# Making the low part of split weights with an accumulating DMA in two token mixers of a two-block transformer kernel

## The chip, the cores and the metric

The kernel runs on one core of one Trainium2 chip, as one launch. The metric is the device time in microseconds (us); lower is better. The engines are called PE (TensorE, matrix products), ACT (ScalarE), DVE (VectorE), POOL (GpSimd) and SP (SyncE, which here only issues DMAs). DMAs are also issued from POOL's and ACT's queues.

## What is computed

Two blocks follow on each other, on 256 tokens of 1024 features. All matrix products are wanted in float32 accuracy.

```python
def first_block(x, c, ctx, c_ctx, ...):      # two layers
    for l in range(2):
        mod = silu(c) @ w_mod[l] + b_mod[l]              # and the same for ctx
        h = rms_norm(x, g_pre_mix[l]) * (1 + sc1) + sh1  # layer 0: x and ctx, 512 tokens; layer 1: x, 256
        y = token_mixer(h, hc, ...)
        x = x + gt1 * rms_norm(y, g_post_mix[l])
        h = rms_norm(x, g_pre_ffn[l]) * (1 + sc2) + sh2
        x = x + gt2 * rms_norm(swiglu(h, w_ffn_in[l], w_ffn_out[l]), g_post_ffn[l])

def token_mixer(h, hc, ...):
    y_a = conformer_conv(h, w_in[:, :1024], ...)         # glu, depthwise convolution of width 31, layer norm
    y_b = differential attention of 8 heads, q, k and v from w_in, rotary positions
    y_c = multiscale_pool(h, w_in[:, 4096:4608], ...)
    g = sigmoid(h @ w_in[:, 4608:] + b_gate)
    return (g_a * y_a + g_b * y_b + g_c * y_c) @ w_out

def second_block(x, mem, positions, ...):    # two layers with other mixers and a swiglu each
```

## The kernel before

The streams lie in SBUF as 8 tiles [128 features, N tokens], with N = 512 in layer 0 of block 1 (x and ctx) and N = 256 from its layer 1 on. A product in float32 accuracy is made of three products in the faster type float32r. Each operand is split into a high part (the value rounded to float32r) and a low part (the value less its high part), and `mm3` (L160 to L166) runs high x high, high x low and low x high into the same PSUM tile. `lin` and `lin_deep` do so with the weights on the stationary side; `lin_nat` (L247 to L249) has them on the moving side.

The weights come as pieces of 128 partitions x 1024 elements, two to a load of 1 MB. `pieces` (L112) gives each piece a function `prep`. The prep of the first piece of a load issues the DMA into `raw`, a ring of two buffers of 1 MB (`RAWS`), from SP's queue (L124). Each prep then rounds its half of `raw` into a tile `whi` with ACT (L154) and writes `raw` less `whi` into a tile `wlo` (L155), on DVE or, for so many pieces in 8 as `SHARE` names for the phase, on POOL. The phase is 0 from the kernel's start to the end of layer 0's mixer, 1 in its ffn, 2 in layer 1's mixer, 3 in its ffn, and 4 to 7 in block 2. In phase 0 POOL subtracts 2 of 8 pieces, in phase 2 none.

Tiles `whi` and `wlo` lie in rings of four (`RING`). `emit` runs the steps of the whole kernel in order and calls a piece's `prep` as early as its ring allows, that is right after the step that uses the piece four before it for the last time. Some pieces of `w_out` in layer 0 use slots in place of the ring (`p.ring`), and some of block 2's weights are permuted (`perm`). Each engine's queue runs in order; the framework lays the queues out and sets all semaphores.

Around the weights a mixer's steps are: the glu's linears, then for four pairs of heads the linears of q, k and v merged with the attention of the pair before (`att_s` scores and softmax, L851 to L861; `att_t` transposes, L882 is the values' product of `att_v`; `rope` at L717 to L725) and with the taps of the convolution (L789 to L795: half of the channels on DVE, the other half scaled on ACT at L792 and added on POOL at L793). After that come the gates, the pooling branch, the output linears of the three branches and `w_out`. In layer 0 modulation products (L476, L478) run on DVE from further loads `mraw`.

Of the kernel before, what the change touches and what calls it, by code (L numbers as in the profile page):

```python
# [6 lines left out]
F32 = mybir.dt.float32  # L7
# [8 lines left out]
T = 256  # L16
# [10 lines left out]
SHARE = (2, 2, 0, 0, 4, 0, 0, 0)  # of 8 weight pieces, how many GpSimd subtracts, by phase  # L27
# [8 lines left out]
class Two:  # L36
    """[128, 8, n] in two tiles"""
# [8 lines left out]
class Kern:  # L46
# [22 lines left out]
    def static(self, tag, n, bufs, dt=F32):  # L69
        """the next of a ring of tiles [128, n] that lie in one"""  # L70
        if tag not in self.rings:
            self.rings[tag] = [self.cp.tile([128, n * bufs], dt, name=tag), 0]
        r = self.rings[tag]
        i = r[1] % bufs
        r[1] += 1
        return r[0][:, n * i:n * i + n]
# [4 lines left out]
    def brief(self, shape, dt=F32):  # L81
        """a small tile out of use before 32 more of its size are in"""
# [28 lines left out]
    def pieces(self, loads, na, nb, cuts, perm=False):  # L111
        box = {}  # L112
        out = []
        for i, (a0, a1, b0, b1) in enumerate(cuts):
# [3 lines left out]
            def prep(p=p, i=i, a0=a0, a1=a1, b0=b0, b1=b1):  # L118
                nc = self.nc
                if i == 0:  # L120
                    raw = self.static("raw", 2048, RAWS)
                    box["raw"] = raw[:, : na * nb].rearrange("p (a b) -> p a b", a=na)
                    for view, src in loads:
                        nc.sync.dma_start(view(box["raw"]), src)  # L124
# [43 lines left out]
    def lin(self, st, W, c0, ncols, rhs, N, evac, perm=False, K=8, tok=None, order=None):  # L168
        """out tile m [128, N] = W[r0:, c0 + 128 m : ...]^T rhs; rhs() -> [(hi, lo)] per k tile.
        tok: a range of the N tokens alone, which evac is told of"""  # L170
# [30 lines left out]
    def lin_pair(self, st, Wa, ca, Wb, cb, n, rhs, N, evac_a, evac_b):  # L201
        """tiles of two column ranges in turn, two by two"""
# [32 lines left out]
    def lin_nat(self, st, W, c0, lhs, ntok, evac):  # L235
        """out [128 tokens, 256 columns]; lhs(t) -> [(hi, lo)] per k tile, [128, 128 tokens]"""
# [50 lines left out]
    def sq_add(self, key, src, N, i, n):  # L287
        """adds src^2 to the running sum self.v[key]"""
# [12 lines left out]
    def col_rms(self, key, nt, dim):  # L301
        """sums over features (partitions) and then 1/rms per token: [128 tokens, nt]"""
# [9 lines left out]
    def bcast(self, r, nt, ps=None, at=0):  # L312
        """[128 tokens, nt] -> PSUM [128, 128 nt]: the same row of tokens on each partition"""
# [119 lines left out]
    def mod(self, l, g):  # L433
        """512 columns on the tensor engine: rows c, c_ctx of the high parts, then of the low parts"""
# [17 lines left out]
    def pin(self, inst):  # L452
        """keeps an instruction that waits for nothing from taking its tile far ahead of its turn"""
# [8 lines left out]
    def mod_v(self, st, l, groups, streams):  # L462
        """the same with the products and their sums over k tiles on the vector engine"""
# [52 lines left out]
    def pre_cols(self, l, s, gain):  # L516
        """(1 + scale) * gain for the two streams: [128, 8, 2]"""
# [13 lines left out]
    def acts(self, n, N):  # L531
        """hi and lo tiles for n k-tiles of N columns"""
# [11 lines left out]
    def act2(self, key, m):  # L544
        """tile m of a run of [128, 256] tiles, allocated two by two"""
# [4 lines left out]
    def norm_mod(self, i, t0, t1, rb, A, sh):  # L550
        """tile i of h from x for tokens t0..t1, whose 1 / rms starts at column 0 of rb"""
# [18 lines left out]
    def y_add(self, m, ps, tok, full):  # L570
        """a tile of the mixer's or the ffn's result: z = gate * gain * y, and the running sums over features of
        y^2, and if full of 2 x z and z^2; the last tile's terms stay apart"""
# [28 lines left out]
    def y_rms(self, t0, full):  # L601
        """1 / rms of y (and if full of the x to come) for 256 tokens: rows 0..255 (256..511) of a PSUM tile"""
# [36 lines left out]
    def residual(self, i, t0):  # L639
        """tile i of x += r * z for 256 tokens"""  # L640
# [7 lines left out]
    def next_h(self, gain):  # L648
        """block 2: the linears take gain * x; 1 / rms of the token follows behind them"""
# [12 lines left out]
    def ffn(self, st, Wgu, Wd, hs, N, evac, rb=None, mid=None):  # L662
        """rb: the tokens' 1 / rms, still missing in hs; the result then lacks it once"""
# [3 lines left out]
        for hi_, (f0, fn) in enumerate(halves):  # L667
# [37 lines left out]
            if mid and hi_ == len(halves) - 1:  # L705
                # by halves of the tokens, the last columns' weights split twice
# [1218 lines left out]
```

## Time and profile before

| | |
|---|---|
| time, median of 3 runs (least to most) | 2356.89 us (2349.86 to 2358.7) |
| profiled execution, first to last instruction | 2355.8 us |
| PE busy | 2197.7 us |
| DVE busy | 1707.7 us |
| ACT busy | 1095.3 us |
| POOL busy | 536.5 us |
| moved by DMA | 319.21 MB |

The profiled execution is one run; its span is what the traces are read against, and no separate time of it outside the profiler is given. Layer 0's mixer lies at about 60 to 615 us, its ffn up to about 1070 us, layer 1's mixer at about 1070 to 1450 us, its ffn up to about 1660 us, and block 2 behind that.

### The profile page before, as it was taken

How to read it: one execution, taken by the hardware profiler on the slowest of the kernel's cores; microseconds unless marked ns; L12 is line 12 of the kernel's file. 1: busy time of each engine (PE TensorE's matmuls, PEld its weight loads, DVE VectorE, ACT ScalarE, POOL GpSimd, SP SyncE). 2: the span in 40 equal slices, each digit the busy share in tenths (PEclk: the TensorE clock that was granted, in tenths of full speed). 3: DMA queues.
4: the chain of work that ended last, by engine and by line, in shares of the span. 5: the costliest groups of instructions: out<-in, count | busy, mean ns of one | idle time of the engine just before them, and what ended most of it. 6: DMA issues, size and time to landing. Idle time of an engine off the chain costs nothing.

```text
span 2355.8 us, 37801 instructions
## 1 busy us (share of the span) xinstructions
PE 2197.7 (93%) x14576; PEld 1998.8 (85%) x14576; DVE 1707.7 (72%) x3443; ACT 1095.3 (46%) x2110; POOL 536.5 (23%) x545
## 2 busy tenths in 40 slices
PE   4978889999989999989999899999889999999998
PEld 3767777788888888878788899999877999988998
DVE  5697987959678745578988877764686766686665
ACT  5436565332332222244566554554446544465543
POOL 2344433321340110143333312100342000210000
PEclk8989999999999999998999999999987999999999
DMA  7312112335414555553322454455541555542553
GB/s 271 93 55 67 54 59 72 123 132 170 152 63 154 168 179 170 170 165 108 108 72 90 148 174 160 154 193 176 160 90 37 176 183 177 177 144 84 185 180 125
DMA packets 296628, 319.21 MB, mean 135 GB/s; under 512 B 20544, under 2 KB 264352, under 8 KB 296448
## 3 DMA queue, kind: packets, MB, share of 16 engines
q1 hardware_dynamic: 293072, 311.27, 41.1%
q0 software_dynamic: 2224, 3.43, 0.6%
q8 instruction: 114, 1.87, 0.3%
q10 hardware_dynamic: 1152, 2.10, 0.3%
q14 instruction: 66, 0.54, 0.1%
HBM read 315.72 MB, written 1.05 MB: 134 GB/s over the span
## 4 chain that ended last, share of the span: by engine, by line
PE 66%; DVE 21%; issue 4%; ACT 3%; DMA 3%; POOL 1%; SPq 0%; ACTq 0%; DVEq 0%; POOLq 0%
PE p L164 19%; PE p L165 19%; PE p L166 19%; DVE wlo L155 3%; DVE t L795 3%; DVE t L478 2%; DVE t L258 2%; PE p L742 1%; DVE b L851 1%; DMA mraw<-in_w_mod_dram 1%; DVE t L725 1%; PE tr L484 1%; DMA raw<-in_w_in_dram 1%; PE p L247 1%; ACT whi L154 1%
## 5 line engine op out<-in xcount | busy, mean ns | idle before, releaser
L164 PE MATMUL p<-t,whi 128*128 128x256 f32 (+1 forms) x3724 | 1175.5, 320 | 20.8 <-ACT t L560 8.5
L165 PE MATMUL p<-t,whi 128*128 128x256 f32 (+1 forms) x3724 | 1183.0, 319 | 5.6 <-DVE t L561 2.1
L166 PE MATMUL p<-t,wlo 128*128 128x256 f32 (+1 forms) x3724 | 1178.2, 318 | 6.4 <-DVE wlo L155 4.8
L164 PEld LDWEIGHTS p<-t,whi 128*128 128x128 f32 x3724 | 718.8, 195 | 72.6 <-ACT t L560 10.3
L165 PEld LDWEIGHTS p<-t,whi 128*128 128x128 f32 x3724 | 723.6, 194 | 50.8 <-DVE t L659 3.5
L166 PEld LDWEIGHTS p<-t,wlo 128*128 128x128 f32 x3724 | 723.1, 194 | 50.4 <-DVE wlo L155 5.9
L154 ACT ACTIVATE whi<-raw 128x1024 fp32r<-128x1024 f32 (+4 forms) x487 | 492.0, 1020 | 543.4 <-PE p L165 332.6
L155 DVE TENSOR_TENSOR wlo<-raw,whi 128x1024 fp32r<-128x1024 f32 (+4 forms) x443 | 545.4, 1232 | 201.7 <-ACT whi L154 113.7
L155 POOL TENSOR_TENSOR wlo<-raw,whi 128x1024 fp32r<-128x1024 f32 (+2 forms) x44 | 103.5, 2353 | 503.6 <-ACT whi L154 464.8
L478 DVE SCALAR_TENSOR_TENSOR t<-mraw,big,t 128x512 f32<-128x512 f32 x224 | 176.6, 827 | 17.7 <-DMA mraw<-in_w_mod_dram 16.2
L793 POOL TENSOR_TENSOR t<-t,t 128x512 f32<-128x512 f32 (+1 forms) x120 | 134.9, 1125 | 186.0 <-ACT t L792 178.5
L594 POOL TENSOR_TENSOR t<-t,t 128x256 f32<-128x256 f32 (+1 forms) x68 | 70.4, 1063 | 246.1 <-ACT t L596 242.8
L299 POOL TENSOR_TENSOR t<-t,t 128x256 f32<-128x256 f32 (+1 forms) x27 | 25.6, 948 | 430.6 <-ACT t L297 430.1
L260 ACT ACTIVATE t<-t 128x256 fp32r<-128x256 f32 (+1 forms) x115 | 54.3, 473 | 148.9 <-DVE t L689 104.4
L742 PE MATMUL p<-t,t 64*128 64x256 f32 (+2 forms) x528 | 78.5, 374 | 28.5 <-DVE t L261 9.8
L247 PE MATMUL p<-whi,t 128*128 128x256 f32 x352 | 101.8, 289 | 2.8 <-ACT t L853 1.6
L248 PE MATMUL p<-wlo,t 128*128 128x256 f32 x352 | 99.8, 284 | 0.0
L249 PE MATMUL p<-whi,t 128*128 128x256 f32 x352 | 99.8, 283 | 0.0
L689 DVE TENSOR_TENSOR t<-t,p 128x256 f32<-128x256 f32 (+1 forms) x91 | 43.1, 474 | 76.8 <-PE p L166 76.6
L795 DVE SCALAR_TENSOR_TENSOR t<-u,big,t 128x512 f32<-128x512 f32 (+1 forms) x120 | 94.9, 791 | 1.5
L742 PEld LDWEIGHTS p<-t,t 64*128 64x128 f32 x528 | 50.9, 206 | 49.2 <-issue 16.8
L257 ACT ACTIVATE t<-t 128x256 fp32r<-128x256 f32 (+1 forms) x92 | 43.2, 495 | 100.0 <-DVE t L725 80.6
(299 smaller groups left out, 2717.0 us busy)
## 6 DMA issues: line engine op xcount, KB each, us to landing
raw<-in_w_in_dram SPq DMA_DIRECT2D x60, 1024.0 KB, 5.1
raw<-in_l_w_gate_up_dram SPq DMA_DIRECT2D x44, 1024.0 KB, 5.1
raw<-in_w_ffn_in_dram SPq DMA_DIRECT2D x42, 1024.0 KB, 5.3
mraw<-in_w_mod_dram SPq DMA_DIRECT2D x80, 512.0 KB, 4.0
raw<-in_l_w_in_dram SPq DMA_DIRECT2D x15, 1024.0 KB, 5.2
raw<-in_l_w_down_dram SPq DMA_DIRECT2D x16, 896.0 KB, 4.9
t<-in_w_mod_dram SPq DMA_DIRECT2D x32, 256.0 KB, 5.4
raw<-in_w_attn_out_dram SPq DMA_DIRECT2D x8, 1024.0 KB, 5.2
```

Of the source, the lines that this page charges most:

```text
L154: nc.scalar.activation(p.hi, src, AF.Copy)
L155: eng.tensor_tensor(p.lo, src, p.hi, op=ALU.subtract)
L164: mm(ps, lh, rh, start=first, stop=False)
L165: mm(ps, lh, rl, start=False, stop=False)
L166: mm(ps, ll, rh, start=False, stop=last)
L247: mm(ps[:, :256], lh, p.hi[:, k % 4], start=k == 0, stop=False)
L248: mm(ps[:, :256], lh, p.lo[:, k % 4], start=False, stop=False)
L249: mm(ps[:, :256], ll, p.hi[:, k % 4], start=False, stop=k == 7)
L478: nc.vector.scalar_tensor_tensor(acc, w[:, k], c, acc, op0=ALU.mult, op1=ALU.add)
L742: self.nc.tensor.matmul(out[half], q[i // 2][h, qs], k[i % 2][h, ks], start=i == 0, stop=i == 2)
L793: nc.gpsimd.tensor_tensor(acc, acc, t, op=ALU.add)
L795: nc.vector.scalar_tensor_tensor(acc, u, w, acc, op0=ALU.mult, op1=ALU.add)
```

## The change

In phases 0 and 2 a piece that has a load of one DMA, the ring of `whi` and `wlo`, and no permutation is prepared in another way. Its load is cut into one DMA for each piece, which writes the piece's weights as one run of 4 KB in each partition of `raw`. ACT writes minus the rounded weights into `wlo` (scale -1), a DMA from POOL's queue adds `raw` to `wlo` in place, and ACT then rounds the weights into `whi` in a second pass. No subtraction is left for these pieces, and the count for `SHARE` does not go on.

```diff
+BY_DMA = (0, 2)
...
                     box["raw"] = raw[:, : na * nb].rearrange("p (a b) -> p a b", a=na)
-                    for view, src in loads:
-                        nc.sync.dma_start(view(box["raw"]), src)
+                    box["dma"] = self.phase in BY_DMA and len(loads) == 1 and not p.ring and not perm
+                    if box["dma"]:
+
+                        at = 0
+                        box["run"] = []
+                        for c0, c1, d0, d1 in cuts:
+                            n = (c1 - c0) * (d1 - d0)
+                            box["run"].append(raw[:, at:at + n])
+                            nc.sync.dma_start(raw[:, at:at + n].rearrange("p (a b) -> p a b", a=c1 - c0),
+                                              loads[0][1][:, c0:c1, d0:d1])
+                            at += n
+                    else:
+                        for view, src in loads:
+                            nc.sync.dma_start(view(box["raw"]), src)
+                if box["dma"]:
+                    src = box["run"][i]
+                    n = src.shape[1]
+                    hi = self.wp.tile([128, 1024], F32R, name=self.nm("whi"), tag="whi", bufs=RING)
+                    lo = self.wp.tile([128, 1024], F32R, name=self.nm("wlo"), tag="wlo", bufs=RING)
+
+                    nc.scalar.activation(lo[:, :n], src, AF.Copy, scale=-1.0)
+                    nc.gpsimd.dma_start(lo[:, :n].bitcast(F32), src, accum_op=ALU.add)
+                    nc.scalar.activation(hi[:, :n], src, AF.Copy)
+                    p.hi = hi[:, :n].rearrange("p (a b) -> p a b", a=a1 - a0)
+                    p.lo = lo[:, :n].rearrange("p (a b) -> p a b", a=a1 - a0)
+                    return
                 src = box["raw"][:, a0:a1, b0:b1]
```

## Rows read from the trace of the kernel before

**Rows 1.** Busy times of the page: busy us, share of the span, instructions.

```profile
PE 2197.7 (93%) x14576; PEld 1998.8 (85%) x14576; DVE 1707.7 (72%) x3443; ACT 1095.3 (46%) x2110; POOL 536.5 (23%) x545
```

**Rows 2.** Busy time of each engine by stretch (from:to, length, then the engines).

```profile
core 0: us, PE busy (x) PEld busy (x) DVE busy (x) ACT busy (x) POOL busy (x), PEclk, DMA share, GB/s
...
110.00:450.00 340.00, 303.07 (x1686) 250.51 (x1685) 291.42 (x571) 176.62 (x401) 140.57 (x106) 0.96 0.20 66
450.00:615.00 165.00, 164.02 (x780) 136.70 (x779) 128.66 (x176) 52.54 (x67) 28.03 (x15) 0.99 0.52 163
...
1110.00:1345.00 235.00, 216.25 (x1523) 197.49 (x1521) 209.92 (x466) 136.02 (x298) 80.06 (x114) 0.96 0.31 101
1345.00:1450.00 105.00, 104.48 (x867) 103.66 (x866) 75.69 (x130) 60.81 (x105) 19.89 (x20) 1.00 0.55 179
```

**Rows 3.** The same for L155, the subtractions: DVE, then POOL.

```profile
110.00:450.00 340.00, 41.96 (x30) 26.27 (x11) 0.96 0.20 66
...
1110.00:1345.00 235.00, 56.91 (x43) 0.00 (x0) 0.96 0.31 101
1345.00:1450.00 105.00, 44.08 (x37) 0.00 (x0) 1.00 0.55 179
```

**Rows 4.** The same for L154, the rounding on ACT.

```profile
110.00:450.00 340.00, 42.11 (x40) 0.96 0.20 66
450.00:615.00 165.00, 29.26 (x28) 0.99 0.52 163
...
1110.00:1345.00 235.00, 46.14 (x44) 0.96 0.31 101
1345.00:1450.00 105.00, 36.16 (x35) 1.00 0.55 179
```

**Rows 5.** Waits of PE, 110 to 450 us: us in total, times, longest.

```profile
PE tr L869 <- DVE t L861: 10.1, 10, 1.8
...
PE tr L925 <- DVE t L923: 0.8, 1, 0.8
```

**Rows 6.** Waits of PE, 1110 to 1345 us.

```profile
PE tr L869 <- DVE t L861: 9.2, 5, 3.8
PE p L164 <- ACT t L260: 3.4, 1, 3.4
...
PE tr L925 <- DVE b L269: 0.2, 1, 0.2
```

**Rows 7.** DMA queue 1, and DMA issues with size and median us to landing.

```profile
q1 hardware_dynamic: 293072, 311.27, 41.1%
...
raw<-in_w_in_dram SPq DMA_DIRECT2D x60, 1024.0 KB, 5.1
...
mraw<-in_w_mod_dram SPq DMA_DIRECT2D x80, 512.0 KB, 4.0
...
t<-in_mem_dram POOLq DMA_DIRECT2D x4, 256.0 KB, 3.5
...
t<-in_k_axc_dram POOLq DMA_DIRECT2D x1, 128.0 KB, 2.3
```

**Rows 8.** Busy times in the first stretches, as in rows 2.

```profile
20.00:30.00 10.00, 8.16 (x34) 6.42 (x34) 7.50 (x13) 5.31 (x12) 1.86 (x5) 1.00 1.05 387
30.00:40.00 10.00, 5.25 (x28) 4.42 (x27) 4.50 (x21) 10.00 (x27) 0.00 (x0) 0.70 1.06 381
```

**Rows 9.** Timeline of DVE and POOL: start, us, instruction.

```profile
1387.10 1.23 DVE L155 TENSOR_TENSOR wlo<-raw,whi 128x1024 fp32r<-128x1024 f32 x1 [2.18 <-ACT whi L154]
...
1258.85 1.67 DVE L155 TENSOR_TENSOR wlo<-raw,whi 128x1024 fp32r<-128x1024 f32 x1
...
1258.71 0.73 POOL L719 TENSOR_TENSOR t<-t,t 128x256 f32<-128x256 f32 x1 [3.34 <-DVE t L717]
```

**Rows 10.** A plain DMA's issue on POOL: ns least, median, most.

```profile
L1301 POOL DMA_DIRECT2D t<-in_mem_dram x4: 543/548/621, 1336.5 to 1338.1; - x4
```

## The prediction, made before the changed kernel ran

> **What bounds the kernel now.** I read the page's busy times first. TensorE (PE) is busy for 93% of the span, VectorE (DVE) for 72% [rows 1]. A share over the whole span hides the stages, so the second view is the table of busy times by stretch, cut at the two mixers that the change touches [rows 2]. The reader should see two kinds of stretch there.
>
> In the first kind, the attention parts (110 to 450 us of layer 0, 1110 to 1345 us of layer 1), PE has gaps: 340 - 303.1 = 37 us and 235 - 216.3 = 19 us. DVE is the busiest engine beside it, 291.4 of 340 us (86%) and 209.9 of 235 us (89%). In the second kind, the dense parts (450 to 615 and 1345 to 1450 us), PE has no gap worth naming: 1.0 and 0.5 us. Nothing that is taken off DVE there can be won.
>
> The third view says whom PE waits for. In 110 to 450 us nine rows name DVE, 35.1 us in all, from 10.1 down to 0.8 us [rows 5]. In 1110 to 1345 us six rows name DVE, 15.5 us in all, and one names ScalarE (ACT), 3.4 us [rows 6]. The releasers are softmax, rope and split instructions, not the weights' own subtraction (2.1 us at most among the six). So the subtractions do harm by standing in DVE's in-order queue ahead of those instructions. About 35 + 15 = 50 us is therefore all that a lighter DVE can give back.
>
> The fourth view is the DMA share by stretch, since the change adds transfers. It is 0.20 and 0.31 in the attention parts, 0.52 and 0.55 in the dense ones [rows 2].
>
> **The change part by part.** From the steps' order about 170 pieces of 128 x 1024 weights take the new path: some 85 in layer 0's mixer (which has phase 0 from the start of the kernel, and whose last steps prepare four pieces of the ffn behind it) and some 85 in layer 1's.
>
> *Removed: the subtraction.* In the attention part of layer 0 DVE loses 42.0 us in 30 instructions and GpSimd (POOL) 26.3 us in 11; in that of layer 1 DVE loses 56.9 us in 43 [rows 3]. A POOL instruction beside it stretches a DVE one: the subtraction took 1.67 us while a POOL addition ran, 1.23 us alone [rows 9]. POOL's 11 subtractions go as well, and at 0.44 us each DVE gets some 4 us more. DVE falls from 86% to (291.4 - 46) / 340 = 72%, and from 89% to (209.9 - 56.9) / 235 = 65%. Its free share goes from 14 to 28% and from 11 to 35%. I take it that a wait behind a queue shrinks about as the free share grows: a half of 35.1 us remains, and a third of 15.5 us. That gives -18 and -10 us. The bounds are 0 (the waits are the length of a chain and not a queue) and -35 and -15.5 us. The start of layer 1's mixer, before 1110 us, still prepares its first four pieces the old way and the next ones the new way: -2 us.
>
> *Added: a second pass of ACT over each piece,* at the price of the pass that is there: 42.1 us / 40, 46.1 / 44, 36.2 / 35, so 1.05 us [rows 4]. ACT goes from 176.6 to 219 of 340 us, from 136.0 to 182 of 235 us, and from 60.8 to 97 of 105 us in layer 1's dense part. Layer 0 has room. In layer 1's attention part PE's 3.4 us of waiting for ACT [rows 6] about doubles: +3 us (bounds 0 and +8). In the dense part ACT is 92% full and still fits. The rounded part now comes 1.05 us later than before, and three pieces of PE time are in hand there (below).
>
> *Added: the accumulating DMA.* No row of before shows one, so its three prices are bounded from plain transfers. First, its issue: POOL's DMA instructions take 0.55 us [rows 10], so 85 of them are 47 us for each layer. That is about what POOL loses in layer 0 and is spread over layer 1, where POOL has 80.1 of 235 us [rows 2]. A POOL instruction behind it waits until the minus pass has been done; these are conv additions and rope additions of a later tile, so I put it at nothing. If that cover fails, a rope addition is late and q or k behind it.
>
> Second, its latency. On the POOL queue 128 KB took 2.3 us and 256 KB 3.5 us to land; on the SP queue 512 KB took 4.0 and 1024 KB 5.1 us [rows 7]. For 512 KB of accumulation I take 4 to 6 us. The low part is then ready 1.05 + 0.55 + 4 to 6, so 5.6 to 7.6 us after the minus pass begins. With rings of four, that pass may begin when the piece four before is used up, three pieces ahead. In the tightest place, the 105 us with 36 pieces (35 and 37 instructions in [rows 3, 4]), a piece takes 2.9 us and the lead is 8.7 us. So it fits, with 1 to 3 us to spare. The rows say little on a POOL transfer of this size. The Trainium skill's page "DMA: Bandwidth & Descriptors" (section "Anatomy of one DMA — SWDGE (gpsimd) path") fits such a DMA as 2.0 us plus its bytes over 436 GB/s; an estimate from that page for 512 KB is 3.2 us, less than the 3.5 us that this trace has for half as much, so the row decides.
>
> Third, its share of the 16 DMA engines. Queue 1 moved 311.27 MB in 41.1% of 2355.8 us [rows 7]: 1.6 us for each 512 KB of plain load. The dense part of layer 1 agrees, 0.55 x 105 / 36 = 1.6 us for each piece. A piece there lasts 2.9 us. Bounds for the accumulation are 0 (it runs beside the loads unseen) and 3.2 us (it reads two operands, each at the price of a load). I take the plain transfer, 1.6 us: 128 rows of 4 KB between two places in SBUF should not be dearer than a load in 1 KB pieces, and the second operand's read may be covered. Then load and accumulation need 3.2 us, and about 40 pieces (36 and the four of the ffn behind them) are 0.3 us late each: +12 us. With 0 it is 0, with 3.2 us it is 40 x (4.8 - 2.9) = +76 us. In layer 0's dense part the DMA engines have 0.52 x 165 = 86 us of work and get 28 x 1.6 = 45 us more. That fits into 165 us: 0 (at 3.2 us, 176 us: +11). In the attention parts 0.20 x 340 + 40 x 1.6 = 132 of 340 us and 0.31 x 235 + 44 x 1.6 = 143 of 235 us fit; at 3.2 us, 214 us still fits.
>
> *Moved: the loads.* Each 1 MB load becomes two of 512 KB in runs of 512 B where they were 1 KB, and the buffer is free only when the accumulation has landed. Two more issues for each pair of pieces are of no weight on a queue that issues one load each 5.8 us here. The loop of a raw half then is: load 4.0, minus pass 1.05, issue 0.55, landing 4 to 6, so 9.6 to 11.6 us against four pieces of 2.9 us = 11.6 us. Closed just in time; nothing is added, and this is the second place where it may fail.
>
> *The start.* Four pieces go the new way in the first 45 us, where the DMA share reaches 1.05 [rows 8]: four passes of ACT of 1.05 us and 4 x 1.6 = 6.4 us of transfers, against four subtractions less. Bounds 0 and +8; I take +2.
>
> The sum: -18 - 10 - 2 + 3 + 12 + 2 = -13 us. The profiled span of 2355.8 us becomes 2343 us, and as the median of the runs lies 1.1 us above that span, the forecast is 2344 us.
>
> **The rivals.** *The DMA engines become the bound.* This ends on the other side. The profile shows for it that a dense piece of layer 1 has only 2.9 - 1.6 = 1.3 us of DMA time free; against it, that stretches with 381 to 387 GB/s exist [rows 8], more than the 179 of the dense part [rows 2] even with the accumulation's bytes added once. Its price is 3.2 us in place of 1.6: -30 + 3 + 76 + 11 + 8 = +68 us at the most, and with some overlap of the two queues about +50: 2407 us. It decides from where the accumulation costs more than about 1.9 us of all engines: 40 x (1.6 + 1.9 - 2.9) = 24 us eats the gain. The Trainium skill's page "Collectives: The Full Stack" (Part 3, "The bandwidth ceiling") says just this: an add inside a DMA costs nothing as arithmetic, but needs two source reads on one read queue and so ran at half the rate of a copy. No row of before shows an accumulation, so the trace neither agrees nor disagrees; because of that rule the rival has a chance as high as it has.
>
> *The waits are chains.* PE's waits for DVE are mostly one instruction long (10.1 us in ten waits, [rows 5]); if they come from softmax steps that follow on each other, a shorter queue gives little, say -12 in place of -30, and the costs of 17 us stay: 2362 us.
>
> *The accumulation is hidden.* With 0 to 1.3 us of engine time nothing is added in the dense part: -30 + 3 + 2 = -25, so 2332 us.
>
> *The low parts come late.* If landing takes 9 us under load, the raw loop is 14.6 us, so 0.75 us for each of 40 pieces: -13 + 30 = +17, 2374 us.
>
> *It does not do what it says* (most pieces would keep the old path): the condition is one load, no ring of slots, no permutation, and only block 2's weights are permuted. I leave it no chance of its own.
>
> **How the numbers follow.** Forecast 0.38, hidden 0.14, chains 0.14, DMA bound 0.28, late 0.06. A measurement of this kernel can tell about 0.5% from no change, 12 us. Around the forecast (2330 to 2356 us) about 0.28 of the 0.38 lies under 2345 us. Faster: 0.28 + 0.14 = 0.42. The same: 0.10 + 0.14 + 0.02 = 0.26. Slower: 0.28 + 0.04 = 0.32. The range reaches from 2318 us (hidden, with two thirds of the waits gone) to 2410 us (the DMA-bound case), leaving out the ends of both. The forecast's own range is 2330 to 2356 us.
>
> **What would show it.** The subtraction should be gone from DVE and POOL in both mixers, and ACT's passes over raw doubled, near 1.05 us. PE's waits for DVE should fall to about 17 and 5 us in the attention parts. In layer 1's dense part the DMA share should rise from 0.55 to above 0.9, and PE should begin to wait for wlo by about 0.3 us a piece. If the DMA share is 1 and PE waits for wlo or raw by 1 us and more a piece, the accumulation reads twice. If the accumulating DMA lands later than 8 us, its latency decides. If PE's waits for DVE stay near 35 us, they were chains. Slower attention parts would prove me wrong outright.

## The result and the profile after

The changed kernel takes 2451.61 us (median; 2447.19 to 2456.9), the kernel before 2354.97 us in the same set of runs: a ratio of 1.0419 [1.04, 1.0438], 96.6 us slower. The forecast was 2344 us with a range up to 2410 us, so both the sign and the range were wrong. The two profiled executions, which all readings below are made from, are 2355.8 and 2445.0 us long, 89.2 us apart.

Line numbers of after lie 25 higher for the old code (`mm3` is L189 to L191, the softmax's last step L886, the transposes L894, the modulation's split L282 and its matmuls L472 and L473, the gates' tanh L934, two other splits L285 and L1059). In the other kernels all lines shift by a few. New lines: L132 the load of one piece, L144 the minus pass, L145 the accumulating DMA, L146 the rounding.

The page's busy times, then the two DMA queues, then the groups of the new lines (count | busy us, mean ns of one | idle before them, and what ended it), then two rows of DMA issues (size and median us to landing). They answer to [rows 1, 7, 10].

```profile
PE 2218.8 (91%) x14576; PEld 2013.3 (82%) x14576; DVE 1494.4 (61%) x3298; ACT 1249.8 (51%) x2280; POOL 604.5 (25%) x690
...
q1 hardware_dynamic: 367120, 311.27, 40.8%
q0 software_dynamic: 26704, 92.05, 20.4%
...
L145 POOL DMA_DIRECT2D wlo<-raw x170 | 149.0, 882 | 403.3 <-ACT wlo L144 354.4
L144 ACT ACTIVATE wlo<-raw 128x1024 fp32r<-128x1024 f32 x170 | 177.7, 1046 | 46.9 <-DMA raw<-in_w_in_dram 27.6
...
wlo<-raw POOLq DMA_DIRECT2D x168, 512.0 KB, 6.4
raw<-in_w_in_dram SPq DMA_DIRECT2D x116, 512.0 KB, 5.9
```

DVE has lost 213 us of work, as was meant, and the new pass of ACT costs what was taken, 1.05 us. The new thing is queue 0, which in before is nearly empty (queue, kind: packets, MB, share of 16 engines):

```profile
q0 software_dynamic: 2224, 3.43, 0.6%
```

20.4% of 2445.0 us less 0.6% of 2355.8 us is 485 us, so one accumulation of 512 KB takes as much time of the DMA engines as all 16 have in 485 / 170 = 2.85 us. Its issue holds POOL for 0.88 us, not 0.55, and it lands after 6.4 us.

Busy times by stretch of after, cut at the same stages as [rows 2] (columns as there):

```profile
core 0: us, PE busy (x) PEld busy (x) DVE busy (x) ACT busy (x) POOL busy (x), PEclk, DMA share, GB/s
130.00:470.00 340.00, 311.59 (x1719) 257.98 (x1719) 237.04 (x548) 219.41 (x449) 146.58 (x146) 0.97 0.59 133
470.00:655.00 185.00, 184.33 (x911) 155.17 (x910) 92.39 (x154) 86.53 (x108) 38.87 (x41) 1.00 1.00 250
1150.00:1375.00 225.00, 212.01 (x1510) 193.81 (x1510) 160.37 (x406) 171.28 (x336) 106.44 (x144) 0.98 0.88 200
1375.00:1540.00 165.00, 128.75 (x912) 123.94 (x910) 31.14 (x85) 95.21 (x144) 48.73 (x63) 0.88 1.04 235
```

The last row is where most of the time went. PE does there in 165 us little more than what took it 105 us before (912 instructions against 867), and the DMA share has gone from 0.55 to 1.04. (The share adds up the packet times of all queues, 64.7% and 39.0% for the two large ones below, so it can pass 1.) The 36.3 us in which PE is idle are told by its waits in that stretch (us in total, times, longest); the waits of ACT and SP, from their own answers, are behind them:

```profile
PE p L191 <- DMA wlo<-raw: 18.4, 15, 2.5
PE p L189 <- ACT t L934: 10.2, 1, 10.2
PE p L189 <- ACT t L1059: 3.8, 1, 3.8
PE p L189 <- ACT t L285: 3.4, 1, 3.4
...
ACT whi L146 <- DMA raw<-in_w_in_dram: 29.3, 6, 13.9
ACT whi L146 <- DMA raw<-in_w_out_dram: 14.0, 6, 5.1
...
SPq L132 <- DMA wlo<-raw: 148.3, 37, 8.4
```

Read from below: SP stands 148 of 165 us until an accumulation lets go of its raw buffer; the load that it then issues is late; ACT stands at the rounding until the load lands; and PE waits for the low part, or for a tanh that stands behind the rounding in ACT's queue. That SP stands is no sign by itself, as it issues each load as soon as a buffer is free. In before it stands too, and there it waits for DVE's subtractions, for instance, in the 135 us from 1345 to 1480 us:

```profile
SPq L124 <- DVE wlo L155: 75.2, 14, 11.3
```

What is new is that the load then comes too late for ACT. One step of the loop in after (start us, length, instruction; idle time before it and what ended it) shows this, and also that the framework has put the rounding (L146) ahead of the minus pass (L144) here; in the whole stretch L146 waits for a load 17 times and L144 three times. So the accumulation begins one pass later than the code reads:

```profile
1467.83 1.06 ACT L146 ACTIVATE whi<-raw 128x1024 fp32r<-128x1024 f32 x1 [4.42 <-DMA raw<-in_w_in_dram]
...
1469.15 1.05 ACT L144 ACTIVATE wlo<-raw 128x1024 fp32r<-128x1024 f32 x1
...
1470.50 0.86 POOL L145 DMA_DIRECT2D wlo<-raw  x1 [5.92 <-ACT wlo L144]
```

The rest of the 60 us is PE itself: its mean instruction took 128.75 / 912 = 0.141 us, 0.1205 us in [rows 2]; on 912 instructions that is 19 us. The granted clock is 0.88 there, a mean between its two levels of 1.2 and 2.4 GHz, in place of 1.00.

The DMA queues of the same stretch (busy tenths of the engines in 40 slices, then the queues, then size and median us to landing of the accumulations and of the largest group of loads; the other groups of loads lie between 5.4 and 7.5 us):

```profile
DMA  9999999989999999999999999999999999999995
...
q0 software_dynamic: 5568, 19.86, 64.7%
q1 hardware_dynamic: 34445, 18.69, 39.0%
...
wlo<-raw POOLq DMA_DIRECT2D x35, 512.0 KB, 7.5
raw<-in_w_in_dram SPq DMA_DIRECT2D x12, 512.0 KB, 8.1
```

Queue 0 moved 19.86 MB, so 38 accumulations of 0.524 MB, and 64.7% of 165 us is 107 us: 2.8 us for each. The price is the same where the engines are full.

To place the whole loss, the starts of five instructions that every kernel here has are read from each trace (lines of before): the first tile of h (L560, the end of the start), the first addition of the convolution's layer norm (L921, right behind the last softmax, once for each layer), the last modulation product of layer 0 (L478), and the last tile of h for layer 1's ffn (L560). The stretches between them, in us:

| kernel | start | attention, layer 0 | dense and ffn, layer 0 | attention, layer 1 | dense, layer 1 | the rest |
|---|---|---|---|---|---|---|
| before | 61.5 | 329.9 | 677.7 | 242.3 | 172.1 | 872.3 |
| after | 86.6 | 329.4 | 686.2 | 239.7 | 232.4 | 870.7 |
| change | +25.1 | -0.5 | +8.5 | -2.6 | +60.3 | -1.6 |

The last column warns of how exact this is: no experiment changes how weights are prepared there (some have a third raw buffer or fewer slots), and it came out between 859.6 and 872.3 us over all of them. So a difference under some 5 us in one stretch is not read, unless the timed comparison bears it out.

The start, last. SP's issues in after (start us, length, instruction), then in before, then one wait of ACT and one of PE in after:

```profile
1.93 6.02 SPq L132 DMA_DIRECT2D raw<-in_w_in_dram  x3
8.40 32.60 SPq L464 DMA_DIRECT2D t<-in_w_mod_dram  x32
41.35 6.41 SPq L132 DMA_DIRECT2D raw<-in_w_in_dram  x4
```

```profile
1.92 1.99 SPq L124 DMA_DIRECT2D raw<-in_w_in_dram  x2
14.46 19.93 SPq L439 DMA_DIRECT2D t<-in_w_mod_dram  x32
```

```profile
ACT wlo L144 <- DMA raw<-in_w_in_dram: 19.1, 1, 19.1
...
PE p L472 <- ACT t L282: 28.8, 7, 18.7
```

In before both 1 MB loads, with the first four pieces, stand ahead of the 32 modulation loads. In after three half loads do, and the fourth comes behind all 32. ACT's queue has the minus pass of that fourth piece ahead of most splits of the modulation weights, so ACT stood 19.1 us for it, and PE 28.8 us for those splits, 6.6 us in before.

### The profile page after: what moved, and what is told of

Same layout as the page of the kernel before. It is cut to its first block, busy times and chain, and to the rows that moved or that the text cites. A ratio compares the mean times of both kernels' runs of the same rounds, so it can differ in the third digit from the quotient of the medians.

```text
span 2445.0 us, 38384 instructions
## 1 busy us (share of the span) xinstructions
PE 2218.8 (91%) x14576; PEld 2013.3 (82%) x14576; DVE 1494.4 (61%) x3298; ACT 1249.8 (51%) x2280; POOL 604.5 (25%) x690
## 3 DMA queue, kind: packets, MB, share of 16 engines
q1 hardware_dynamic: 367120, 311.27, 40.8%
q0 software_dynamic: 26704, 92.05, 20.4%
HBM read 315.72 MB, written 1.05 MB: 130 GB/s over the span
## 4 chain that ended last, share of the span: by engine, by line
PE 59%; DVE 14%; DMA 10%; ACT 5%; issue 5%; POOL 3%; ACTq 0%; SPq 0%; DVEq 0%; POOLq 0%
PE p L189 17%; PE p L191 17%; PE p L190 17%; DMA wlo<-raw 3%; DVE t L820 2%; DMA raw<-in_w_in_dram 2%; DMA mraw<-in_w_mod_dram 1%; PE p L767 1%; DVE wlo L180 1%; DVE t L283 1%; PE p L272 1%; DVE t L503 1%; PE p L273 1%; PE p L274 1%; PE tr L907 1%
## 5 line engine op out<-in xcount | busy, mean ns | idle before, releaser
L189 PE MATMUL p<-t,whi 128*128 128x256 f32 (+1 forms) x3724 | 1186.0, 323 | 53.9 <-ACT t L934 10.2
L191 PE MATMUL p<-t,wlo 128*128 128x256 f32 (+1 forms) x3724 | 1186.8, 320 | 29.4 <-DMA wlo<-raw 23.9
L189 PEld LDWEIGHTS p<-t,whi 128*128 128x128 f32 x3724 | 726.3, 197 | 107.4 <-ACT t L585 10.6
L191 PEld LDWEIGHTS p<-t,wlo 128*128 128x128 f32 x3724 | 729.8, 196 | 78.0 <-DMA wlo<-raw 28.5
L190 PEld LDWEIGHTS p<-t,whi 128*128 128x128 f32 x3724 | 730.8, 197 | 48.1 <-DVE t L586 3.1
L179 ACT ACTIVATE whi<-raw 128x1024 fp32r<-128x1024 f32 (+3 forms) x317 | 313.9, 1002 | 319.3 <-PE p L190 168.8
L180 DVE TENSOR_TENSOR wlo<-raw,whi 128x1024 fp32r<-128x1024 f32 (+3 forms) x294 | 352.6, 1201 | 138.9 <-PE p L191 74.1
L146 ACT ACTIVATE whi<-raw 128x1024 fp32r<-128x1024 f32 x170 | 178.0, 1049 | 198.6 <-PE p L190 73.9
L145 POOL DMA_DIRECT2D wlo<-raw x170 | 149.0, 882 | 403.3 <-ACT wlo L144 354.4
L144 ACT ACTIVATE wlo<-raw 128x1024 fp32r<-128x1024 f32 x170 | 177.7, 1046 | 46.9 <-DMA raw<-in_w_in_dram 27.6
L503 DVE SCALAR_TENSOR_TENSOR t<-mraw,big,t 128x512 f32<-128x512 f32 x224 | 165.2, 778 | 52.6 <-DMA mraw<-in_w_mod_dram 51.2
L285 ACT ACTIVATE t<-t 128x256 fp32r<-128x256 f32 (+1 forms) x115 | 54.2, 471 | 143.4 <-DVE t L714 111.6
L180 POOL TENSOR_TENSOR wlo<-raw,whi 128x1024 fp32r<-128x1024 f32 (+2 forms) x23 | 50.6, 2201 | 310.6 <-ACT whi L179 238.4
L767 PE MATMUL p<-t,t 64*128 64x256 f32 (+2 forms) x528 | 76.6, 372 | 27.5 <-DVE t L743 9.1
```

The source lines that it names most:

```text
L144: nc.scalar.activation(lo[:, :n], src, AF.Copy, scale=-1.0)
L145: nc.gpsimd.dma_start(lo[:, :n].bitcast(F32), src, accum_op=ALU.add)
L146: nc.scalar.activation(hi[:, :n], src, AF.Copy)
L179: nc.scalar.activation(p.hi, src, AF.Copy)
L180: eng.tensor_tensor(p.lo, src, p.hi, op=ALU.subtract)
L189: mm(ps, lh, rh, start=first, stop=False)
```

## The experiments

Each is the changed kernel with the edit shown, unless it is said otherwise. Ratios are against the kernel before, timed beside it.

**The start alone undone.** The first four pieces are prepared the old way.

```diff
+        self.new = False
...
-                    box["dma"] = self.phase in BY_DMA and ...
+                    box["dma"] = self.new and self.phase in BY_DMA and ...
...
-            st += mix
+            st += mix[:1] + [X(lambda: setattr(self, "new", True), 0)] + mix[1:]
```

> The changed kernel, but the first four pieces of the whole kernel are prepared the old way (one 1 MB load for two, subtraction on DVE or POOL). In the changed kernel the start is 25 us late. Theory A: a load cut in two puts the fourth half behind 32 modulation loads on SP's queue, and ACT's in-order queue stands still for it (19 us); then this run gains about 25 us: 2427 us. Theory B: the start is late by the bytes of four accumulations in a stretch where the DMA engines are full, 4 x 2.85 = 11 us: 2440 us.

Measured: 2420.98 us, ratio 1.0276 [1.0257, 1.0295], 30.6 us less than after. The start is 60.8 us again, the dense part of layer 1 still 233.8 us. The loss at the start stands by itself and the loss in the dense part does not come from it.

**The new way in the attention parts alone.** As the edit above, and `self.new` is set to False where the pooling linears begin.

```diff
+        out.append(("x", 0, lambda: setattr(self, "new", False)))
         pl = []
         self.lin(pl, W, 4096, 512, hx, N, pool_evac)
```

> The changed kernel with the new way only in the attention part of each mixer: the first four pieces, and all from the pooling linear on, are prepared the old way. Theory: the 97 us are the start (25), the dense part of layer 1 (62) and a part of what lies behind layer 0's attention (13), all from the DMA engines and the queues; without them the small gain of the attention parts stays, some 9 us: 2346 us. Rival: the attention parts pay too, as the low parts and raw buffers come later, and their gain is chance: 2355 us or above.

Measured: 2341.64 us, ratio 0.9932 [0.9909, 0.9954]: faster than before. The dense part of layer 1 is 173.6 us; the attention parts are 325.1 and 236.1 us, -4.8 and -6.2. So where the DMA engines have room the change pays, but these parts gain 11 us of the 27 that the prediction gave them.

**Without the accumulating DMA.** `wlo` stays at minus the rounded weights, so the low part lacks the weights themselves; the rest is as after.

```diff
                     nc.scalar.activation(lo[:, :n], src, AF.Copy, scale=-1.0)
-                    nc.gpsimd.dma_start(lo[:, :n].bitcast(F32), src, accum_op=ALU.add)
                     nc.scalar.activation(hi[:, :n], src, AF.Copy)
```

> The changed kernel without the accumulating DMA: the low part stays minus the rounded weights (so the output is another), and everything else is as in the changed kernel, the split loads and both passes of ACT. Theory: the DMA engines make the dense part of layer 1 slow, so its 62 us vanish; the start keeps its 25 us if they come from the split loads. If PE's waits in the attention parts are queues behind DVE, these parts gain 28 us here and the time is about 2355 us; if they are chains, about 9 us as in the changed kernel: 2374 us. If ACT's second pass were the bound of the dense part, 2410 us or more would stay.

Measured: 2333.87 us, ratio 0.9908 [0.9893, 0.9924], although the start is late here too (81.6 us). The attention parts take 314.9 and 229.8 us, so -15.0 and -12.5 us: 27.5 us together, as the prediction's lighter queue wanted. The two passes of ACT do no harm in the dense part of layer 1, 168.4 us. The time is 21 us under the expectation: the dense parts, from which nothing was expected, read 8.1 and 3.7 us shorter than before, and the start is 5 us less late than in after. No run explains the 8.1 us. Busy times by stretch of this kernel (columns as above), with the attention and the dense part of layer 1:

```profile
1125.00:1330.00 205.00, 199.88 (x1448) 182.58 (x1448) 147.18 (x384) 162.85 (x322) 70.66 (x98) 1.00 0.38 110
1330.00:1430.00 100.00, 97.24 (x796) 96.47 (x795) 30.06 (x82) 86.06 (x132) 12.31 (x17) 0.98 0.57 170
```

ACT is 86% busy in the second row, and PE has gaps of 2.8 us. What after loses, apart from its start, hangs on the accumulating DMA (its time on the engines, its landing and its issue together; this run does not part them).

**The split loads alone.** Two half loads, but rounding and subtraction as before.

```diff
-                    nc.scalar.activation(lo[:, :n], src, AF.Copy, scale=-1.0)
-                    nc.gpsimd.dma_start(lo[:, :n].bitcast(F32), src, accum_op=ALU.add)
+                    self.load += SHARE[self.phase]
+                    eng = nc.gpsimd if self.load >= 8 else nc.vector
+                    self.load %= 8
                     nc.scalar.activation(hi[:, :n], src, AF.Copy)
+                    eng.tensor_tensor(lo[:, :n], src, hi[:, :n], op=ALU.subtract)
```

> The changed kernel with its split loads into two runs, but one pass of ACT and the old subtraction on DVE and POOL, no accumulating DMA. Theory A (the start is late because of the order on SP's queue): about 20 to 25 us late at the start, and nothing else: 2378 us. Theory B (the accumulations' bytes): as before, 2356 us. The runs of 512 B in place of 1 KB should raise the DMA time of a load from 1.63 to about 1.8 us for 512 KB, which nothing waits for here.

Measured: 2376.61 us, ratio 1.009 [1.0075, 1.0105]. The start is 80.5 us, +19.0; that is 19 of the 22.4 us lost against the kernel before beside it (2354.26 us). So most of the late start is the order of the loads, not the accumulation. The attention parts read 3.7 and 5.5 us longer, which the stretches can't tell from nothing: in the control below, which prepares everything the old way, layer 1's attention part reads 5.3 us longer than in before.

**A copy in place of the addition.** The DMA moves the same bytes but does not add, so the low part is the weights themselves.

```diff
-                    nc.gpsimd.dma_start(lo[:, :n].bitcast(F32), src, accum_op=ALU.add)
+                    nc.gpsimd.dma_start(lo[:, :n].bitcast(F32), src)
```

> The changed kernel with the DMA from POOL's queue as a plain copy of raw over wlo, without the addition (so the low part is the whole weight, and the output is another). In the changed kernel queue 0 takes 2.85 us of all 16 engines for each 512 KB. Theory (the second operand's read is the price): the copy takes 1.4 to 1.6 us, a dense piece of layer 1 needs 1.8 + 1.5 = 3.3 us against 2.9 us, so that part loses 15 us and not 60; with the start still late, 2395 us. Rival (rows from SBUF to SBUF on that queue cost this much whatever the operation): 2.85 us again and 2450 us.

Measured: 2387.74 us, ratio 1.0137 [1.0118, 1.0157], 64 us less than after. Its queue 0, POOL's issues and the landing (columns as in after):

```profile
q0 software_dynamic: 26576, 92.05, 10.5%
...
L145 POOL DMA_DIRECT2D wlo<-raw x170 | 94.2, 554 | 387.8 <-ACT wlo L144 355.8
...
wlo<-raw POOLq DMA_DIRECT2D x168, 512.0 KB, 4.2
```

(0.105 x 2387.0 - 14) / 170 = 1.39 us of all engines: the accumulation costs 2.05 times a copy of the same bytes, and its issue 0.88 us where the copy's is 0.55. The Trainium skill's page "Collectives: The Full Stack" (Part 3, "The bandwidth ceiling") has it that an add inside a DMA needs two source reads and so runs at half a copy's rate. An estimate by that rule from the copy's 1.39 us is 2.78 us, and the trace agrees with 2.85. The dense part of layer 1 takes 194.1 us with copies, 38 us less than with accumulations and still 22 us more than before, at a DMA share of 0.90 and 290 GB/s:

```profile
1345.00:1490.00 145.00, 130.35 (x1012) 125.75 (x1011) 43.24 (x113) 106.18 (x162) 45.21 (x74) 0.97 0.90 290
```

So even a little below the price that the prediction took, the dense part loses nearly twice the 12 us of its sum. The accumulation's price on the engines is not all of it.

**A third raw buffer, in the attention-only version and in after.**

```diff
-SLOTS, RING, MORE, RAWS, US, MRAWS = 66, 4, 4, 2, 6, 2
+SLOTS, RING, MORE, RAWS, US, MRAWS = 66, 4, 4, 3, 6, 2
```

The attention-only version:

> The kernel with the new way in the attention parts alone, with three raw buffers in place of two. Without the accumulating DMA these parts gain 15 and 12 us, with it 5 and 6. Theory (raw comes free late, since the accumulation lands late, and ACT's queue stands still for the next load): a third buffer gives back most of the rest, some 10 us: 2332 us. Rival (the bytes themselves, shared engines): 2341 us as with two.

Measured: 2323.04 us, ratio 0.9863 [0.9845, 0.9881], 18.6 us less than with two buffers. The attention parts are 319.4 and 232.2 us, -10.5 and -10.1. That places 9.6 of the 17.1 us between the two profiled runs; the others lie in stretches with the old way, at most 3.3 us in one, which is under what a stretch can tell.

All of after:

> The changed kernel with three raw buffers in place of two. Theory (the DMA engines are full in the dense part of layer 1): more buffers give no bandwidth, that part stays 60 us late and the time is 2435 to 2450 us. Rival (the loop of load, minus pass, issue and landing over two raw buffers is the bound): the dense part gains 30 us or more, 2415 us or less.

Measured: 2420.0 us, ratio 1.0278 [1.0259, 1.0298]; the dense part of layer 1 is 214.8 us. That lies between the two expectations: some 18 of its 60 us went with the loop through the raw buffer, and 43 stay. Its row and its queues over that part:

```profile
1355.00:1520.00 165.00, 134.10 (x982) 128.76 (x981) 44.20 (x110) 103.49 (x158) 57.75 (x75) 0.92 1.06 247
```

```profile
DMA  9759999999999999999999999999999999999999
...
q0 software_dynamic: 5865, 20.95, 64.2%
q1 hardware_dynamic: 35882, 19.61, 41.5%
```

The engines are full from the fourth slice on. If a second operand's read is counted for the accumulation as well, (2 x 20.95 + 19.61) MB / 165 us = 373 GB/s, against the 381 to 387 GB/s of the fullest stretches in [rows 8]. In after the same count is 354 GB/s.

**The control: the kernel before with a third raw buffer.** It needs the room of four slots, so the attention-only version was run with 62 slots too.

```diff
-SLOTS, RING, MORE, RAWS, US, MRAWS = 66, 4, 4, 2, 6, 2
+SLOTS, RING, MORE, RAWS, US, MRAWS = 62, 4, 4, 3, 6, 2
```

The kernel before:

> The kernel before, everything done the old way, with a third raw buffer (and 62 slots instead of 66, to make room for it). Theory: what the third raw buffer gave the version with the change in the attention parts alone (2341.6 to 2323.0 us) came from the loop that the accumulation lengthens (a raw buffer is free only when the accumulation that reads it has ended), so the old way, whose subtraction frees the buffer, gains little: 2345 to 2360 us. Rival: the third buffer simply lets every load run earlier, and gives the old way as much: 2330 to 2340 us.

The attention-only version:

> The version with the change in the attention parts alone and three raw buffers, here with 62 slots instead of 66, so that it differs from the old way with three raw buffers in the change alone. If the four slots are worth nothing: 2318 to 2328 us, as with 66. If the slots are what the elementwise engines run ahead into: 2335 us or more.

Measured: 2354.27 us, ratio 1.0002 [0.9987, 1.0018], for the old way, and 2324.01 us, ratio 0.9863 [0.984, 0.9886], for the attention-only version. The buffer by itself gives nothing, and the four slots cost nothing. So the third buffer's 18 us come only together with the change. That it shortens the loop that the accumulation lengthens fits this, though only 9.6 us of it could be placed in the attention parts. With three buffers on both sides the change is worth 30 us where it pays.

**Every third load of the dense parts.** The attention-only version, with `self.third` set where `self.new` ends:

```diff
+                    self.loads += 1
+                    box["dma"] = (self.new or self.third and self.loads % 3 == 0) and self.phase in BY_DMA and ...
```

With two raw buffers:

> The new way in the attention parts, and behind them for every third load. DMA time for three loads in layer 1's dense part: 6 x 1.7 + 2 x 2.9 = 16 us against 6 x 2.9 = 17.4 us of PE. Theory (only full DMA engines make it slow): the dense part loses little, 0 to 5 us, and gains nothing, since PE has no gaps there: 2342 to 2347 us. Rival (each late low part costs by its own latency): a third of 60 us, 2362 us.

With three:

> The change in the attention parts and on every third load of the dense parts, with three raw buffers instead of two. With two it was 2368 us and the dense stretch of layer 1 took 190.4 us against 173.6 us without those loads, though q1 and q0 together filled only 72% of the DMA engines there. Theory (the loop of a raw buffer is too long for its third of the loads, the engines are not full): the third buffer takes most of the 17 us away, the dense stretch of layer 1 is at 170 to 177 us and the kernel at 2323 to 2335 us. Rival (the accumulation's traffic itself slows the loads): the stretch stays at 183 us or more and the kernel at 2340 us or more.

Measured: 2368.12 us, ratio 1.006 [1.0038, 1.0083], and 2344.92 us, ratio 0.9957 [0.9942, 0.9972]. The first is more than even its rival expected (2362 us). With two buffers the dense part of layer 1 is 190.4 us, 17 us over the attention-only version; queue 1 takes 48.4% and queue 0 28.5% of the engines there, 77% together, and SP waits for accumulations in few but long stretches (us in total, times, longest; L141 is the whole load there, so loads of the old way stand behind accumulations):

```profile
SPq L141 <- DMA wlo<-raw: 91.0, 9, 15.8
```

With three buffers it is 177.3 us, 7 us over. So the third buffer takes 10 of the 17 us, on engines that were not full. The whole kernel is still 22 us over the attention-only version with three buffers, 7 of them in this part. Neither expectation for three buffers covers that: the stretch went nearly with the first (170 to 177 us), the total with the second (2340 us and more). No run parts these 22 us further.

**Whole loads.** The attention-only version with three raw buffers; the load stays whole, and accumulation and passes read their half out of it, for 64 of the 80 pieces in runs of 512 B (the 16 of the values' weights, `lin_nat`, keep one run of 4 KB).

```diff
...
-                            nc.sync.dma_start(raw[:, at:at + n].rearrange("p (a b) -> p a b", a=c1 - c0),
-                                              loads[0][1][:, c0:c1, d0:d1])
...
+                        nc.sync.dma_start(box["raw"], loads[0][1])
+                        box["run"] = [box["raw"][:, c0:c1, d0:d1] for c0, c1, d0, d1 in cuts]
...
```

> The change in the attention parts alone with three raw buffers, but with the raw load whole, 1 MB in one DMA as before the change, where a weight was split into two loads of 512 KB; the accumulation then reads 512-byte runs out of it. The split loads alone cost the attention parts 3.7 and 5.5 us when the subtraction was kept. Theory (the split is a cost of its own): about 9 us less than the 2323 us with split loads, 2312 to 2318 us. Rival (the split pays here, since the first half's passes and its accumulation start while the second half is under way, and a strided source makes the accumulation dearer than 2.85 us a piece): 2325 to 2340 us.

Measured: 2343.25 us, ratio 0.9946 [0.9927, 0.9964], 20 us more than with split loads. The attention parts are 327.9 and 244.7 us. First this kernel (L141 is its accumulation), then the one with split loads:

```profile
q0 software_dynamic: 71088, 45.38, 15.2%
...
L141 POOL DMA_DIRECT2D wlo<-raw x80 | 115.2, 1488 | 92.7 <-ACT wlo L140 81.8
...
wlo<-raw POOLq DMA_DIRECT2D x80, 512.0 KB, 7.7
```

```profile
q0 software_dynamic: 13744, 45.38, 10.6%
...
wlo<-raw POOLq DMA_DIRECT2D x80, 512.0 KB, 5.8
```

The same bytes in five times the packets: (0.152 x 2339.2 - 14) / 80 = 4.27 us of the engines for a piece, against 2.90, and an issue of 1.49 us. These are means over both kinds of piece. With 2.90 us for each of the 16, the 64 others cost (342 - 46) / 64 = 4.6 us; their issues take 1.56 us, those of the 16 0.87. So the split, whose issues the prediction counted as of no weight, keeps the accumulation at its price, and away from the start it pays for itself. How much of the 20 us is that price, and how much that a first half can't start before the whole load has landed, was not tried.

## Why the prediction was wrong

Its sum beside the stretches (the term for the start of layer 1's mixer and ACT's term lie in layer 1's attention):

| term | predicted, us | after | without the accumulating DMA | attention only, three raws |
|---|---|---|---|---|
| start | +2 | +25.1 | +20.1 | +0.8 |
| attention, layer 0 | -18 | -0.5 | -15.0 | -10.5 |
| attention, layer 1 | -10 - 2 + 3 | -2.6 | -12.5 | -10.1 |
| dense and ffn, layer 0 | 0 | +8.5 | -8.1 | -1.4 |
| dense, layer 1 | +12 | +60.3 | -3.7 | -1.8 |

*The bound and the waits were read right.* DVE's queue did hold back PE in the attention parts. Without the accumulation they gave 27.5 us for a predicted 27 (18 + 10 + 2 - 3). That the sum fits so closely is partly luck: layer 0 gave 15.0 us for 18, layer 1 12.5 for 9, and in layer 0 PE's waits for DVE fell to 23.1 us in that run and not to 17. PE's waits for DVE in after are 27.0 and 4.5 us, for 35.1 and 15.5 in [rows 5, 6] and 17 and 5 forecast; two rows of after's waits, one from each part:

```profile
PE tr L894 <- DVE t L886: 9.9, 9, 2.6
...
PE tr L894 <- DVE t L886: 2.8, 3, 1.7
```

In layer 0 the softmax row of after stays near the 10.1 us that it had, and without the accumulation it is still 7.3 us, so much of that row looks like a chain and not a queue, as the rival had it; the rival as a whole, with 12 us of relief, is refuted by the 27.5.

*The step that failed first: the accumulation's share of the DMA engines.* The prediction bounded it by 0 and 3.2 us and took 1.6, arguing that a transfer inside SBUF is no dearer than a load and that the second operand's read may be covered. The first half is right (a copy measures 1.39 us), the second is wrong: the addition measures 2.85 us. At the prediction's own formula this gives 40 x (1.6 + 2.85 - 2.9) = 62 us for the dense part of layer 1, and it measured 60.3. The rival that named this mechanism had the decision point (1.9 us) and the place right, but its 2407 us still fall 45 us short: it left the attention parts a relief of 30 us and gave the start 8 us at most. Its argument against itself, that 381 GB/s exist, counted the accumulation's bytes once; with both reads counted the dense part would have needed 179 + 2 x 181 = 541 GB/s (0.524 MB each 2.9 us is 181), which no stretch shown here has. In layer 0's dense part the bound of 3.2 us gave +11, and the stretch has +8.5.

*The agreement of 62 with 60.3 is partly luck.* Copies in place of additions take 38 us from it, so that much hangs on the addition; the copies at 1.39 us still cost 22 us. And the third buffer takes 18 us from it, which full engines alone would not allow. The loop through the raw buffer, "closed just in time" at 9.6 to 11.6 us for 11.6, did not close. Its terms were all taken at the light end: load 4.0 us, measured 5.4 to 8.1 in that stretch as medians; landing 4 to 6, measured 7.5; issue 0.55, measured 0.88; and the second pass of ACT, which stands ahead of the minus pass there, was not in it. The prediction added nothing for it and gave its failure a chance of 0.06. The two causes are not apart either: a full engine lengthens load and landing, and these the loop.

*The second step: the start.* It was costed by the work that it does (four passes, 6.4 us of transfers) and not by the order in the queues. With the loads split, the framework put one of the four halves behind 32 other loads in SP's queue, although the code issues the two halves of a load side by side, and ACT's queue had a pass that needs it ahead of others that PE waits for. +2 became +25; 19 of it come with the split alone, 20 with the split and the passes but no accumulation. The prediction's bound of +8 left that out.

*The third: the attention parts don't keep their relief.* That they had room for the transfers (143 of 235 us) was right as a mean: the DMA share in after is 0.59 in layer 0's and 0.88 in layer 1's. But the transfers come in bursts, as the busy tenths of the engines from 130 to 440 us of the attention-only version show:

```profile
DMA  9666843653198355228835520768565374340404
```

In a burst the raw buffer is taken to be the limit. The third buffer points to it: in the attention-only version -4.8 becomes -10.5 us in layer 0 and -6.2 becomes -10.1 in layer 1, in all of after layer 0 goes from -0.5 to -9.4 us (320.5), while the old way gains nothing from the buffer. In layer 1 of after it gives nothing that can be told (239.3 us); there the DMA share is 0.88. What keeps the 20.6 us of the best version from the 27.5 us without the DMA was not tried.

*What stays open.* The granted clock in the dense part fell from 1.00 to 0.88 where PE was idle for 22% of the time; no run gave PE the clock without the waits, so the 19 us of slower instructions count with the waits, and how much of them is the clock is not shown. Three raw buffers with copies were not run, so the 22 us that copies cost are not parted either. 7 us of the 96.6 are between the medians and the profiled pair.

*The better version.* The change in the attention parts alone, split loads and three raw buffers: 2323.04 us, ratio 0.9863 [0.9845, 0.9881], faster than both.

## What to carry to other kernels

Count an accumulating DMA as two copies of its bytes on the DMA engines (2.85 against 1.39 us here), and add it to the loads of the densest stretch before anything else is counted: it can stand in for a subtraction only where loads and accumulations together leave the engines room. Whoever makes a buffer live longer (here raw, until a DMA that reads it has landed) has to go through the loop of that buffer with loaded latencies and give it another buffer. Splitting a DMA gives the framework one more instruction to place, and its place need not be beside the first half; look in the trace at what stands between, in the issuing queue and in the queue of the engine that waits for it.

## What the runs showed of the hardware

- An addition inside a DMA, SBUF to SBUF, 512 KB in runs of 4 KB: 2.85 us of all 16 engines, 6.4 us to land under this load, 0.88 us of issue on POOL. A copy of the same bytes: 1.39, 4.2 and 0.55 us. The Trainium skill's page "DMA: Bandwidth & Descriptors" (section "Anatomy of one DMA — SWDGE (gpsimd) path") has a formula by which an estimate for 512 KB to land is 3.2 us. Both measure more, and the measurement decides.
- The same addition with its source in runs of 512 B: 4.6 us of the engines (an estimate from the mean of 4.27 over 80 pieces, 64 of them in such runs), 1.56 us of issue, and 7.7 us to land as the median of all 80.
- Cutting the loads of 170 pieces in two, most of them into runs of 512 B where they were 1 KB, cost little: queue 1 took 998 us in after (367120 packets) and 968 us in before (293072) for the same 311.27 MB.
